# Value weights in buffers of their own, all early transfers asked for in order of use, aligned token rows, and another order of the last small operations

## The chip, the core and the metric

The kernel runs on one core of a Trainium2 chip. The time is the device time of one execution in microseconds. The profile's span is the stretch from the first to the last instruction in it; the profiled execution's own time is longer by what lies around the span. The engines are PE (matrix multiplication; PEld is its weight load), DVE (vector), ACT (scalar), POOL (general) and SP (asks for most transfers; ACT has a DMA queue of its own). PE works out of SBUF into eight banks of PSUM.

## The reference

256 tokens of width 1024 pass two layers. Everything is float32.

```
h = x
hn = rms_norm(h, g[0,0]);  h = h + stick_breaking_attention(hn, w_qkv, w_o)   # 16 heads of 64
h = h + sqrelu_mlp(rms_norm(h, g[0,1]), w1, w2)                               # 1024 -> 4096 -> 1024
shared = nsa_shared_kv(h, kv_norm, w_kv, cmp_pos, cmp_w1, cmp_w2)             # K/V of three branches
hn = rms_norm(h, g[1,0]);  h = h + nsa_attention(hn, w_q, gate_b, w_o, shared)
h = h + sqrelu_mlp(rms_norm(h, g[1,1]), w1, w2)
return rms_norm(h, final_norm)
```

In the first attention `qkv = hn @ w_qkv` with `w_qkv` of 1024 x 3072; its last third gives the values, 256 x 1024. Both ends of this program are what the change is about: the value projection, with which the kernel begins, and the final norm.

## The kernel before

A float32 product is made of three matmuls in a rounded type: each operand is split into a high part (`wh`, `xa` as `xn[0]`) and the remainder (`wl`, `xn[1]`), and high x high, low x high and high x low are added up in PSUM. For weights, `wh` is a cast, mostly on ACT, and `wl = raw - wh` a subtraction on DVE (`split`).

All weights form one list, `stream`, in the order of their use. `fetch` asks for the next entry on SP's queue and makes the coroutine that splits it. Raw weights lie in three buffers in turn (`tag="raw"`), split ones in three (`NB`). The next `fetch` is made when the second `wl` of a block has been issued, so a request stands on SP until DVE has freed the buffer.

The order of the instructions on DVE, ACT and POOL is set at build time by a planner (`Order`, `Chain`): it keeps a clock of its own, with costs such as `150 + 1.045 * m` for DVE, gives every chain of operations a rank and the time at which its data is expected (`ws.landed`), and issues whatever its model says can run. Each engine then runs its list in that order. PE's order is written out by hand.

`layer0` begins with eight matmuls on constants. Then the value projection runs over the eight blocks k of 128 input features: `v_first` for k=0 (two weight entries, `i_v0`, 512 columns each), `v_proj(i)` for the others, in pieces given by `V_CUT` as pairs (first k, how many k). For each k it takes the token rows, transposed, 128 features x 256 tokens (`xraw` from `in_xt`; `turned(k)` multiplies by the norm's gain and splits into `xa`) and twelve matmuls of 128x512 into four banks `pv`. `load(k0, k1)` asks for token rows: each row of `in_xt` begins with eight gains and goes on with 8 x 256 tokens, so block k begins at 32 + 1024 k bytes in a row of 8224. After the last k come `pr` (the row norms spread over a tile), and then `proj`, the q and k projections from `in_wqk`, one entry of 1024 KB for each pair of heads.

At the end of the second MLP `finish` is called for each finished quarter (token block t, column half n; the last quarter in two pieces of 256 columns). It issues the residual's square on ACT with a sum, the product with the final gain on DVE (`gain`), the running sum (`part`), and, after the last piece of a token block, the power -1/2 on POOL, the scaling by it in three pieces (384 columns on ACT, two of 320 on DVE) and three output transfers.

Of the kernel before, what the change touches and what calls it, by code (L numbers as in the profile page):

```python
# [8 lines left out]
F32 = mybir.dt.float32  # L9
# [18 lines left out]
V_CUT = ((1, 1), (2, 1), (3, 1), (4, 1), (5, 1), (6, 2))  # L28
# [143 lines left out]
def hybrid_kernel(ctx, tc, x, xt, eye, gcols, gfin, wqk, wv, wo0, wkv, wvs, wq, wg, wo1, w1, w2, cw1, cw2, cpos, gate_b, consts, out):  # L172
# [18 lines left out]
    def slot(i, shape, dt, name):  # L191
        return cp.tile(shape, dt, tag=f"e{i}", name=name, bufs=1)
# [51 lines left out]
    class Weights:  # L244
        raws, made, parts, gone, cur, landed = [], [], [], 0, -1, 0.0

    ws = Weights()
    ways = {"hi": "A"}

    def fetch():  # L250
        j = len(ws.raws)
        if j == len(stream):
            return
        src, n, whole = stream[j]
        raw = wp.tile([P, n], F32, tag="raw", name="raw", bufs=3)
        ws.raws.append(raw)
        ws.made.append(None)
        cuts = 2 if j == 0 else 1
        for c in range(cuts):
            r = slice(c * n // cuts, (c + 1) * n // cuts)  # L260
            nc.sync.dma_start(raw[:, r], src[:, r])
        for h in range(2):
            if h < cuts:
                ws.landed = max(o.t + 1900, ws.landed) + P * n * 4 / cuts / 330
            ws.parts.append(Chain(o, whole_part(j, h) if whole else split(j, h), rank_of(j), ws.landed))
# [9 lines left out]
    def split(j, half):  # L275
# [30 lines left out]
        if half:  # L306
            fetch()
# [246 lines left out]
    def layer0(ap):  # L554
# [6 lines left out]
        xg = slot(1, [P, NK + NK * T * P], F32, "xraw")  # L561
        xraw = xg[:, NK:].rearrange("p (k q) -> p k q", k=NK)
# [11 lines left out]
        def load(k0, k1):  # L574
            a, b = NK * (k0 > 0) + k0 * T * P, NK + k1 * T * P
            (nc.sync if k0 else nc.scalar).dma_start(xg[:, a:b], xt[:, a:b])
            ws.landed = max(o.t + 1900, ws.landed) + P * (k1 - k0) * 1024 / 330
            for k in range(k0, k1):
                in_x[k] = Chain(o, turned(k), 0.4, ws.landed)
# [31 lines left out]
        fetch()  # L611
        load(1, 2)
        fetch()
        load(2, 4)
        nc.scalar.dma_start(gc, gcols)
# [5 lines left out]
        load(4, 8)  # L621
# [6 lines left out]
        ws.landed = max(o.t + 1900, ws.landed) + 4500  # L628
        rstd = [None, None]
        rc = [Chain(o, rstd_of(t, rstd), 1.5, ws.landed) for t in range(T)]  # L630
# [3 lines left out]
        v_proj(5)  # L634
# [768 lines left out]
    last, gained = [[], []], [[], []]  # L1403
    ends = [[(0, 512)]] * 3 + [[(0, 256), (256, 512)]]

    def finish(i, q, c):
# [21 lines left out]
        def gen():  # L1428
            yield c
            gained[t].append(go(gain(), 0.3, 0))  # L1430
            yield act(m, lambda: nc.scalar.activation(sq[:, q], hres[t][:, q], AF.Square, accum_out=ss[:, k:k + 1]), 190)
            if k:
                yield last[t][k - 1]
            yield dve(1, lambda: nc.vector.tensor_scalar(part, ss[:, k:k + 1], part if k else D * EPS, None, op0=OP.add))
            if end:
                yield pool(1, lambda: nc.gpsimd.tensor_tensor(part, part, npow, op=OP.pow), 370)
# [43 lines left out]
def _layout(inp):  # L1480
# [6 lines left out]
    def blocks(w, nk, cw):  # L1487
# [14 lines left out]
        "xt": cont(np.concatenate([a["norm_gain"].reshape(4, D)[0].reshape(NK, P).T, a["x"][0].T.reshape(NK, P, T * P).transpose(1, 0, 2).reshape(P, NK * T * P)], 1)),  # L1502
# [39 lines left out]
```

## Time and profile before

| | us |
|---|---|
| median of 3 runs (lowest, highest) | 623.21 (623.17, 623.98) |
| time of the profiled execution | 623.1 |
| its span | 621.0 |
| PE busy in the span | 610.7 |
| DVE, ACT busy | 424.5, 328.3 |
| mean granted clock of PE, share of full | 0.998 |

In the views that follow a row of the timeline is: start, length, engine, line, operation, output<-input, shapes, how many were merged (x4), and in brackets the idle time of that engine just before and what ended it. A row "SPq" or "ACTq" is the time an engine takes to ask for transfers. "PE busy" lets a matmul end some 0.2 us after the next has begun, so the distance between starts, not the length, tells what one matmul costs. Requests of 128 x n float32 are n/2 KB.

### The profile page before, as it was taken

To read this page: it belongs to the slowest core of one execution; us is meant where nothing else is said; L and a number is where in the kernel's file an instruction comes from. 1 tells how busy PE (TensorE), PEld (TensorE's weight loads), DVE (VectorE), ACT (ScalarE), POOL (GpSimd) and SP (SyncE) were. 2 spreads that over 40 slices of the span, in tenths; PEclk is the share of its full clock that TensorE was granted. 3 is DMA by queue.
4 is the path that set the end of the run, shared out by engine and by line. 5 is a ranking of instruction groups with operands and counts; after the bars stand their busy time and mean duration, and the time that the engine had idled before them with its cause. 6 is when DMAs were issued, how large, how long until landed. Compare 5 with 4: busy or idle time off the path is not lost.

```text
span 621.0 us, 8967 instructions
## 1 busy us (share of the span) xinstructions
PE 610.7 (98%) x3580; PEld 513.4 (83%) x3580; DVE 424.5 (68%) x615; ACT 328.3 (53%) x563; POOL 41.2 (7%) x57
## 2 busy tenths in 40 slices
PE   8999999999999999999999999999999999999995
PEld 5799997888888888888887788677888888888884
DVE  4688996686656666555938999873876665566655
ACT  4657675464555444543906776452654554444432
POOL 0000000000000000000111542310000000000000
PEclk9999999999999999999999999999999999999999
DMA  7974425255554545555355363112365555455501
GB/s 260 369 283 158 142 99 179 86 220 195 203 205 172 188 183 203 204 176 218 140 203 204 136 204 137 69 69 102 137 218 197 194 194 212 163 191 189 204 1 68
DMA packets 17898, 108.24 MB, mean 174 GB/s; under 512 B 2368, under 2 KB 4160, under 8 KB 5696
## 3 DMA queue, kind: packets, MB, share of 16 engines
q1 hardware_dynamic: 17280, 107.11, 47.5%
q8 instruction: 28, 0.46, 0.3%
q10 hardware_dynamic: 576, 0.55, 0.3%
q14 instruction: 14, 0.11, 0.0%
HBM read 106.61 MB, written 1.05 MB: 173 GB/s over the span
## 4 chain that ended last, share of the span: by engine, by line
PE 82%; DVE 10%; DMA 3%; ACT 2%; issue 2%; SPq 0%; POOLq 0%; POOL 0%; DVEq 0%; ACTq 0%
PE acc L347 34%; PE pu L347 29%; PE qk L347 7%; DVE wl L299 4%; PE pk L347 4%; PE po L347 3%; PE z L347 2%; DMA raw<-in_wqk 1%; DVE nm L1084 1%; PE qp L347 1%; PE pt L359 1%; PE pa L359 1%; PE ptp L359 1%; DMA raw<-in_wv 1%; DMA xraw<-in_xt 1%
## 5 line engine op out<-in xcount | busy, mean ns | idle before, releaser
L299 DVE TENSOR_TENSOR wl<-raw,wh 128x1024 fp32r<-128x1024 f32 (+2 forms) x196 | 227.8, 1185 | 110.1 <-ACT wh L293 110.0
L293 ACT CAST wh<-raw 128x1024 fp32r<-128x1024 f32 (+2 forms) x196 | 193.9, 1018 | 116.7 <-PE acc L347 46.3
L347 PE MATMUL pu<-xn,wh 128*128 128x512 f32 x512 | 130.7, 394 | 0.0
L347 PEld LDWEIGHTS pu<-xn,wh 128*128 128x128 f32 x512 | 93.3, 188 | 18.7 <-issue 0.5
L347 PE MATMUL acc<-wh,hh 128*128 128x512 f32 (+1 forms) x256 | 99.7, 389 | 0.0
L347 PE MATMUL acc<-wl,hh 128*128 128x512 f32 (+1 forms) x256 | 99.6, 389 | 0.0
L347 PE MATMUL acc<-wh,hl 128*128 128x512 f32 (+1 forms) x256 | 99.4, 388 | 0.0
L347 PEld LDWEIGHTS pu<-xn,wl 128*128 128x128 f32 x512 | 70.8, 189 | 6.1
L347 PE MATMUL pu<-xn,wl 128*128 128x256 f32 x512 | 72.4, 281 | 0.0
L347 PEld LDWEIGHTS acc<-wh,hl 128*128 128x128 f32 x256 | 48.0, 188 | 10.0
L347 PEld LDWEIGHTS acc<-wh,hh 128*128 128x128 f32 x256 | 48.1, 188 | 9.1
L347 PEld LDWEIGHTS acc<-wl,hh 128*128 128x128 f32 x256 | 48.2, 188 | 8.9
L513 ACT CAST hh<-ms 128x512 fp32r<-128x512 f32 x32 | 19.9, 622 | 61.3 <-DVE ms L512 61.3
L347 PE MATMUL qk<-xa,wh 128*128 128x256 f32 x256 | 46.8, 285 | 0.0
L347 PE MATMUL acc<-wh,oT 128*128 128x512 f32 x128 | 43.7, 404 | 0.7 <-DVE oT L437 0.7
L347 PEld LDWEIGHTS qk<-xa,wh 128*128 128x128 f32 x256 | 39.2, 189 | 0.5 <-issue 0.3
L347 PE MATMUL qk<-xa,wl 128*128 128x256 f32 x128 | 36.1, 282 | 0.6 <-DVE wl L299 0.6
L499 ACT COPY mr<-pu 128x256 f32<-128x256 f32 x64 | 23.6, 369 | 24.2 <-PE pu L347 24.2
L514 DVE TENSOR_TENSOR hl<-ms,hh 128x512 fp32r<-128x512 f32 x32 | 22.1, 692 | 19.4 <-ACT hh L513 19.4
L347 PE MATMUL pk<-wh,xk 128*128 128x512 f32 (+1 forms) x128 | 33.6, 342 | 0.0
L1078 ACT ACTIVATE pe<-z,nm 128x256 f32<-128x256 f32 (+1 forms) x64 | 26.1, 428 | 12.7 <-DVE nm L1084 12.6
L347 PEld LDWEIGHTS acc<-wh,oT 128*128 128x128 f32 x128 | 24.0, 188 | 6.7 <-DVE oT L437 0.9
(178 smaller groups left out, 731.7 us busy)
## 6 DMA issues: line engine op xcount, KB each, us to landing
raw<-in_w SPq DMA_DIRECT2D x64, 1024.0 KB, 4.8
raw<-in_wqk SPq DMA_DIRECT2D x8, 1024.0 KB, 5.6
raw<-in_wo SPq DMA_DIRECT2D x8, 1024.0 KB, 4.8
raw<-in_wkv SPq DMA_DIRECT2D x4, 1024.0 KB, 4.9
raw<-in_cw SPq DMA_DIRECT2D x4, 1024.0 KB, 4.8
raw<-in_wq SPq DMA_DIRECT2D x4, 1024.0 KB, 4.9
raw<-in_wv SPq DMA_DIRECT2D x5, 512.0 KB, 5.0
raw<-in_wvs SPq DMA_DIRECT2D x2, 1024.0 KB, 5.0
```

Source lines behind the costliest of these rows:

```text
L293: nc.scalar.copy(ws.made[j][0][:, r], ws.raws[j][:, r])
L299: nc.vector.tensor_sub(ws.made[j][1][:, r], ws.raws[j][:, r], f32(ws.made[j][0][:, r]))
L347: nc.tensor.matmul(o_, a, b, start=first, stop=last, skip_group_check=True)
L359: nc.tensor.transpose(o_, a, i)
L499: yield act(256, lambda: nc.scalar.copy(r[:, q], pu[f][:, 256:512]))
L513: yield act(512, lambda: nc.scalar.copy(hh, sv))
L514: yield dve(512, lambda: nc.vector.tensor_sub(hl, sv, f32(hh)), port=True)
L1078: return act(n, lambda: nc.scalar.activation(d, z, AF.Exp, bias=nm[:, i:i + 1], accum_out=rs[:, t, hd, b:b + 1]), 150)
L1084: yield dve(256 * (t + 1), lambda: nc.vector.tensor_reduce(nm[:, i:i + 2], z, axis=AX.X, op=OP.max, negate=True))
```

## The change

Before the first matmul that needs data, the program now asks for all value weights, all token rows, the gains `gc`, x itself and the constants, and for three qk entries. The entries of the value weights have buffers of their own (`rv0` to `rv6`, in the pool of `layer0`), so they no longer wait for DVE; from the qk entries on the three `raw` buffers are used as before. Token rows of k=0 and k=1 go on ACT's queue, those of k=2 to 7 in pairs on SP's, between the weights. `gc` moves from ACT's queue to SP's. k=4 and k=5 form one entry; the third entry and the last two are asked for in two halves. The row of `in_xt` is filled up to 64 values ahead of the tokens, so a block begins at 256 + 1024 k bytes in a row of 8448. `lands` is a new model of when a transfer lands, for the planner only. In `finish`, the gains of a token block's last piece are issued after the running sum, and the scaling is one piece of 704 columns on DVE and 320 on ACT, with two transfers.

```diff
-V_CUT = ((1, 1), (2, 1), (3, 1), (4, 1), (5, 1), (6, 2))
+V_CUT = ((1, 1), (2, 1), (3, 1), (4, 2), (6, 2))
...
+    def lands(n):
+        ws.path = max(ws.path, o.t + 1100)
+        ws.path += n / (270 if ws.path < 10000 else 390)
+        ws.landed = ws.path + 1300
...
-        raw = wp.tile([P, n], F32, tag="raw", name="raw", bufs=3)
+        if j in i_v0 or j in i_v:
+            raw = ws.pool.tile([P, n], F32, name=f"rv{j}", bufs=1)
+        else:
+            raw = wp.tile([P, n], F32, tag="raw", name="raw", bufs=3)
-        cuts = 2 if j == 0 else 1
+        cuts = 2 if j in (0, 2) or j in i_v[-2:] else 1
...
-        if half:
+        if half and j > i_v[-1]:
             fetch()
...
-        xg = slot(1, [P, NK + NK * T * P], F32, "xraw")
+        xg = slot(1, [P, DH + NK * T * P], F32, "xraw")
...
-            (nc.sync if k0 else nc.scalar).dma_start(xg[:, a:b], xt[:, a:b])
+            (nc.sync if k0 > 1 else nc.scalar).dma_start(xg[:, a:b], xt[:, a:b])
...
         load(0, 1)
         fetch()
-        fetch()
         load(1, 2)
         fetch()
+        fetch()
         load(2, 4)
-        nc.scalar.dma_start(gc, gcols)
+        fetch()
+        fetch()
+        load(4, 6)
+        fetch()
+        load(6, 8)
+        fetch()
+        nc.sync.dma_start(gc, gcols)
+        for t in range(T):
+            nc.sync.dma_start(hres[t], x[t * P:(t + 1) * P, :])
+        nc.sync.dma_start(ident, eye)
+        nc.sync.dma_start(cst[:, 0:C_ROT], consts[:, 0:C_ROT])
...
+        for _ in range(3):
+            fetch()
...
         v_proj(1)
-        for t in range(T):
-            nc.sync.dma_start(hres[t], x[t * P:(t + 1) * P, :])
-        nc.sync.dma_start(ident, eye)
-        nc.sync.dma_start(cst[:, 0:C_ROT], consts[:, 0:C_ROT])
...
         def gen():
             yield c
-            gained[t].append(go(gain(), 0.3, 0))
+            late[t].append(gain)
+            if not end:
+                gained[t].append(go(late[t].pop()(), 0.3, 0))
...
             if end:
+                gained[t].extend(go(g(), 0.2, 0) for g in late[t])
...
-                yield [scaled("A", 640, 1024), scaled("D", 0, 320)]
-                yield [scaled("D", 320, 640)]
+                yield [scaled("A", 704, 1024), scaled("D", 0, 704)]
```

How this moves instructions, at three places. First SP's queue at the start of the program. In brackets stand the semaphores that a request waits for: DMAHW0 to DMAHW7 are eight counters that transfers take in turn and raise when they land, DVE_49 counts DVE's instructions. Before:

```order
L261 DMA raw_97<-in_wv 128x256 x2
L261 DMA raw_100<-in_wv 128x512
L576 DMA xraw_91<-in_xt 128x256
L261 DMA raw_103<-in_wv 128x1024
L576 DMA xraw_91<-in_xt 128x512
L261 DMA raw_125<-in_wv 128x1024 [waits DMAHW1_49,DMAHW0_49,DVE_49]
L261 DMA raw_138<-in_wv 128x1024 [waits DMAHW2_49,DVE_49]
L576 DMA xraw_91<-in_xt 128x1024
L261 DMA raw_160<-in_wv 128x1024 [waits DMAHW6_49,DMAHW3_49,DVE_49]
L261 DMA raw_182<-in_wv 128x1024 [waits DMAHW4_49,DMAHW0_49,DVE_49]
```

After:

```order
L269 DMA rv0_97<-in_wv 128x256 x2
L269 DMA rv1_101<-in_wv 128x512
L269 DMA rv2_103<-in_wv 128x512 x2
L585 DMA xraw_91<-in_xt 128x512
L269 DMA rv3_107<-in_wv 128x1024 [waits DMAHW0_49]
L269 DMA rv4_109<-in_wv 128x1024 [waits DMAHW1_49]
L585 DMA xraw_91<-in_xt 128x512 [waits DMAHW2_49]
L269 DMA rv5_112<-in_wv 128x1024 [waits DMAHW3_49]
L269 DMA rv5_112<-in_wv 128x1024 [waits DMAHW4_49]
L585 DMA xraw_91<-in_xt 128x512 [waits DMAHW5_49]
L269 DMA rv6_116<-in_wv 128x1024 [waits DMAHW6_49]
L269 DMA rv6_116<-in_wv 128x1024 [waits DMAHW7_49]
```

The token rows of k=1 (128x256) have left this queue, and no request there waits for DVE any more, only for the transfer eight places ahead of it.

Second, ACT at the same place: its two requests, then its first casts. Before:

```order
L576 DMA xraw_91<-in_xt 128x264
L615 DMA gc_70<-in_gcols 128x48
L293 CAST wh_111<-raw_97 128x256 [waits DMAHW0_49]
L293 CAST wh_111<-raw_97 128x256 [waits DMAHW1_49]
L293 CAST wh_121<-raw_100 128x256 [waits DMAHW2_49]
L293 CAST wh_121<-raw_100 128x256
L293 CAST wh_141<-raw_103 128x512 [waits DMAHW6_49]
L293 CAST wh_141<-raw_103 128x512
L568 ACTIVATE xa_89<-xraw_91 128x256 [waits DMAHW7_49,DMAHW3_49]
```

After:

```order
L585 DMA xraw_91<-in_xt 128x320
L585 DMA xraw_91<-in_xt 128x256
L301 CAST wh_135<-rv0_97 128x256 [waits DMAHW0_49]
L301 CAST wh_135<-rv0_97 128x256 [waits DMAHW1_49]
L577 ACTIVATE xa_89<-xraw_91 128x256 [waits DMAHW4_49,DMAHW3_49]
L301 CAST wh_152<-rv1_101 128x256 [waits DMAHW2_49]
L301 CAST wh_152<-rv1_101 128x256
L301 CAST wh_159<-rv2_103 128x512 [waits DMAHW5_49]
L301 CAST wh_159<-rv2_103 128x512 [waits DMAHW6_49]
```

The first operation on token rows k=1, which was DVE's (a TENSOR_SCALAR ahead of the second block's `wl`), is now ACT's, ahead of the second block's casts.

Third, DVE at the end, from the last quarter on. Before:

```order
L445 SCALAR_TENSOR_TENSOR hres1_73<-accz_5537,r2_4724,hres1_73 128x256 [waits DVE_49,PE_49]
L1434 TENSOR_SCALAR ssq1_4115<-ssq1_4115 128x1 [waits Activation_49]
L1425 SCALAR_TENSOR_TENSOR ys1_4117<-hres1_73,gf_4112 128x256
L1425 SCALAR_TENSOR_TENSOR ys1_4117<-hres1_73,gf_4112 128x256 [waits DVE_49]
L1434 TENSOR_SCALAR ssq1_4115<-ssq1_4115 128x1 [waits DVE_49,Activation_49]
L1420 TENSOR_SCALAR ys1_4117<-ys1_4117,ssq1_4115 128x320 [waits Pool_49]
L1420 TENSOR_SCALAR ys1_4117<-ys1_4117,ssq1_4115 128x320 [waits DVE_49]
```

After:

```order
L453 SCALAR_TENSOR_TENSOR hres1_73<-accz_5531,r2_4720,hres1_73 128x256 [waits DVE_49,PE_49]
L1451 TENSOR_SCALAR ssq1_4111<-ssq1_4111 128x1 [waits Activation_49]
L1440 SCALAR_TENSOR_TENSOR ys1_4113<-hres1_73,gf_4108 128x256
L1451 TENSOR_SCALAR ssq1_4111<-ssq1_4111 128x1 [waits DVE_49,Activation_49]
L1440 SCALAR_TENSOR_TENSOR ys1_4113<-hres1_73,gf_4108 128x256
L1435 TENSOR_SCALAR ys1_4113<-ys1_4113,ssq1_4111 128x704 [waits Pool_49]
```

One gain has gone behind the running sum, and one scaling has taken the place of two. PE's own order is the same from end to end. Between the two ends, the orders of DVE, ACT and POOL are the same but for layer 1, where the planner's clock has come to other choices: over the whole program one product `qw` has gone from POOL to DVE, one copy `pT` from DVE to ACT, and one half of `pe` from DVE to POOL.

More of the change, by code (lines that the diff above doesn't have):

```diff
@@ L244, in hybrid_kernel @@
     class Weights:
-        raws, made, parts, gone, cur, landed = [], [], [], 0, -1, 0.0
+        raws, made, parts, gone, cur, landed, path, pool = [], [], [], 0, -1, 0.0, 0.0, None
     ws = Weights()
     ways = {"hi": "A"}
+    def lands(n):
+        ws.path = max(ws.path, o.t + 1100)
+        ws.path += n / (270 if ws.path < 10000 else 390)
+        ws.landed = ws.path + 1300
     def fetch():
@@ L263, in fetch @@
             if h < cuts:
-                ws.landed = max(o.t + 1900, ws.landed) + P * n * 4 / cuts / 330
+                lands(P * n * 4 // cuts)
             ws.parts.append(Chain(o, whole_part(j, h) if whole else split(j, h), rank_of(j), ws.landed))
@@ L560, in layer0 @@
         v = slot(0, [P, T, D], F32, "v0")
-        xg = slot(1, [P, NK + NK * T * P], F32, "xraw")
-        xraw = xg[:, NK:].rearrange("p (k q) -> p k q", k=NK)
+        ws.pool = ap
+        xg = slot(1, [P, DH + NK * T * P], F32, "xraw")
+        xraw = xg[:, DH:].rearrange("p (k q) -> p k q", k=NK)
         pv = [[B(2 * n + t, f"pv{t}{n}") for n in range(2)] for t in range(T)]
@@ L574, in load @@
         def load(k0, k1):
-            a, b = NK * (k0 > 0) + k0 * T * P, NK + k1 * T * P
-            (nc.sync if k0 else nc.scalar).dma_start(xg[:, a:b], xt[:, a:b])
-            ws.landed = max(o.t + 1900, ws.landed) + P * (k1 - k0) * 1024 / 330
+            a, b = DH * (k0 > 0) + k0 * T * P, DH + k1 * T * P
+            (nc.sync if k0 > 1 else nc.scalar).dma_start(xg[:, a:b], xt[:, a:b])
+            lands(P * (k1 - k0) * 1024)
             for k in range(k0, k1):
@@ L610, in layer0 @@
         fetch()
-        fetch()
         load(1, 2)
         fetch()
+        fetch()
         load(2, 4)
-        nc.scalar.dma_start(gc, gcols)
+        fetch()
[9 more added lines that the diff above has]
+        nc.sync.dma_start(cst[:, 0:C_ROT], consts[:, 0:C_ROT])
+        lands(1250000)
+        rstd = [None, None]
+        rc = [Chain(o, rstd_of(t, rstd), 1.5, ws.landed) for t in range(T)]
+        for _ in range(3):
+            fetch()
         go_on = ap.tile([P, 2 * ROW], BF16, name="go_on", bufs=1)
@@ L620, in layer0 @@
         v_first(1)
-        load(4, 8)
         v_proj(0)
         v_proj(1)
-        for t in range(T):
-            nc.sync.dma_start(hres[t], x[t * P:(t + 1) * P, :])
-        nc.sync.dma_start(ident, eye)
-        nc.sync.dma_start(cst[:, 0:C_ROT], consts[:, 0:C_ROT])
-        ws.landed = max(o.t + 1900, ws.landed) + 4500
-        rstd = [None, None]
-        rc = [Chain(o, rstd_of(t, rstd), 1.5, ws.landed) for t in range(T)]
         v_proj(2)
@@ L633, in layer0 @@
         v_proj(4)
-        v_proj(5)
         o.need(*rc)
@@ L1402, in hybrid_kernel @@
     ys = [slot(1 + t, [P, 2, D], F32, f"ys{t}") for t in range(T)]
-    last, gained = [[], []], [[], []]
+    last, gained, late = [[], []], [[], []], [[], []]
     ends = [[(0, 512)]] * 3 + [[(0, 256), (256, 512)]]
@@ L1501, in _layout @@
         "x": cont(a["x"][0]),
-        "xt": cont(np.concatenate([a["norm_gain"].reshape(4, D)[0].reshape(NK, P).T, a["x"][0].T.reshape(NK, P, T * P).transpose(1, 0, 2).reshape(P, NK * T * P)], 1)),
+        "xt": cont(np.concatenate([a["norm_gain"].reshape(4, D)[0].reshape(NK, P).T, np.zeros((P, DH - NK), np.float32), a["x"][0].T.reshape(NK, P, T * P).transpose(1, 0, 2).reshape(P, NK * T * P)], 1)),
         "eye": np.eye(P, dtype=np.float32),
```

## The prediction

> **What bounds the kernel now.** I read the page's first part, then the list of what each engine waited for, then the timeline of the two ends. The first row of the page:
>
> ```profile
> PE 610.7 (98%) x3580; PEld 513.4 (83%) x3580; DVE 424.5 (68%) x615; ACT 328.3 (53%) x563; POOL 41.2 (7%) x57
> ```
>
> PE (the matmuls) is busy for 610.7 of 621.0 us. Whatever shortens the kernel must close a gap of PE, and there are few. The waits of PE over the whole span (us in total, times, longest):
>
> ```profile
> PE pv L347 <- DVE wl L299: 1.3, 1, 1.3
> ...
> PE acc L347 <- DVE oT L437: 0.7, 1, 0.7
> PE qk L347 <- DVE wl L299: 0.6, 1, 0.6
> PE ptp L359 <- DVE pT L1131: 0.2, 1, 0.2
> ```
>
> The first and third lie in the first 31 us, where the diff works; the others lie in layer 1. Now the first gap, in the timeline (start, length, engine, operation; in brackets what ended the idle time before it):
>
> ```profile
> 1.19 0.45 ACTq L615 DMA_DIRECT2D gc<-in_gcols  x1
> ...
> 2.11 0.43 SPq L576 DMA_DIRECT2D xraw<-in_xt  x1
> ...
> 5.29 0.72 ACT L293 CAST wh<-raw 128x256 fp32r<-128x256 f32 x2 [0.56 <-DMA raw<-in_wv]
> ...
> 6.09 1.15 PE L347 MATMUL pv<-wh,xa 128*128 128x512 f32 x4
> 7.06 0.35 DVE L569 TENSOR_SCALAR xa<-xraw 128x256 fp32r<-128x256 f32 x1 [1.63 <-DMA xraw<-in_xt]
> ...
> 8.06 0.42 DVE L299 TENSOR_TENSOR wl<-raw,wh 128x256 fp32r<-128x256 f32 x1
> 8.34 1.15 ACT L293 CAST wh<-raw 128x512 fp32r<-128x512 f32 x2 [2.33 <-DMA raw<-in_wv]
> 8.53 0.73 PE L347 MATMUL pv<-wl,xa 128*128 128x512 f32 x2 [1.28 <-DVE wl L299]
> ...
> 9.11 1.11 PE L347 MATMUL pv<-wh,xa 128*128 128x512 f32 x4
> 9.39 0.51 ACT L568 ACTIVATE xa<-xraw 128x256 fp32r<-128x256 f32 x1
> ...
> 11.92 1.09 PE L347 MATMUL pv<-wh,xa 128*128 128x512 f32 x4
> ```
>
> The two wl halves of the second weight block stand on DVE behind the first operation on token row block k=1, whose transfer, asked for at 2.1, lands only at 7.0. PE needs the last of them at 7.03 (6.09 and four matmuls of 0.233: from 9.11 to 11.92 twelve take 2.81) and gets it at 8.5. So k=1 begins at 9.1, k=2 at 11.92, and from there PE runs without a wait to the end of the value projection. Then the second gap:
>
> ```profile
> 22.50 1.06 ACT L381 ACTIVATE sq<-hres 128x1024 f32<-128x1024 f32 x1
> ...
> 27.75 1.99 ACT L293 CAST wh<-raw 128x1024 fp32r<-128x1024 f32 x2 [3.06 <-DMA raw<-in_wqk]
> 28.83 1.22 DVE L299 TENSOR_TENSOR wl<-raw,wh 128x1024 fp32r<-128x1024 f32 x1 [3.96 <-ACT wh L293]
> 29.07 0.48 PE L347 MATMUL qk<-xa,wh 128*128 128x256 f32 x2
> 30.11 0.39 PE L347 MATMUL qk<-xa,wl 128*128 128x256 f32 x1 [0.55 <-DVE wl L299]
> 30.33 0.40 PE L347 MATMUL qk<-xa,wh 128*128 128x256 f32 x2
> 30.57 0.28 PE L347 MATMUL qk<-xa,wl 128*128 128x256 f32 x1
> ```
>
> The first block of the qk weights lands at 27.7, and its first wl comes 2.4 us later, at 30.11. Two wh matmuls take 0.24 (30.33 to 30.57), so without a wait the wl matmul would have begun at 29.07 + 0.24 = 29.31: 0.8 us are lost there (the list counts 0.6, since it lets the matmuls before end late). What the transfers did meanwhile (busy time of each engine in a stretch; the last two numbers are the share of the 16 DMA engines and GB/s):
>
> ```profile
> 0.00:6.80 6.80, 5.99 (x21) 3.08 (x22) 1.51 (x4) 2.81 (x5) 1.10 (x7) 1.00 0.66 196
> 6.00:8.50 2.50, 1.25 (x6) 0.67 (x4) 1.42 (x4) 0.17 (x2) 0.00 (x0) 1.00 1.01 385
> 9.00:10.00 1.00, 1.00 (x6) 0.85 (x5) 1.00 (x3) 0.89 (x2) 0.00 (x0) 1.00 0.45 90
> 10.00:20.00 10.00, 10.00 (x44) 7.95 (x44) 8.26 (x17) 5.48 (x10) 0.00 (x0) 1.00 0.90 317
> 0.00:25.50 25.50, 23.41 (x95) 16.60 (x96) 14.87 (x31) 13.93 (x24) 2.20 (x11) 1.00 0.85 302
> 20.00:30.00 10.00, 9.56 (x45) 7.62 (x43) 3.84 (x7) 6.34 (x9) 1.23 (x5) 1.00 1.03 422
> 340.00:395.00 55.00, 54.07 (x431) 44.05 (x430) 53.28 (x103) 37.87 (x110) 24.18 (x18) 1.00 0.45 158
> ```
>
> And one transfer by itself (size, us from request to landing):
>
> ```profile
> gc<-in_gcols ACTq DMA_DIRECT2D x1, 24.0 KB, 3.3
> ```
>
> The stream runs dry at 9 to 10 us (90 GB/s): the weights have three buffers, and each further request waits for DVE to free one.
>
> **The change, part by part.** All times below are on the profiled span, 621.0, of an execution of 623.1; the median of the runs is 623.2, 0.1 above.
>
> (1) First gap. Three arrivals decide it. (a) Token rows k=1 go from the fourth place on SP to the second on ACT's queue, where gc lands at 1.19 + 3.3 = 4.5:
>
> That queue now carries 295 KB instead of 160, 135 more; at half of 385 GB/s, since SP's queue moves beside it, 0.7 us: landing at 5.2 (4.9 if it had all; 7.0 at worst, as now). ACT, not DVE, now takes the first operation on k=1 and stands there before it casts the second weight block: 5.2 + 0.05 + 0.5 (the ACTIVATE of 0.51) + 0.8 (5.29 to 6.09, two casts until PE starts) gives 6.55 for the four wh matmuls, 0.45 later than now; the wl are then in time, and k=0 ends at 6.55 + 0.93 + 0.47 = 7.95. (b) The third weight block, in two requests: its first half is complete after 131 + 131 + 262 + 164 + 131 + 262 = 1081 KB. The old stream had 196 x 6.8 = 1333 KB through at 6.8, so 1081 at 6.15. It had the old third block through at 6.8 (1339 KB) and ACT took it at 8.3, a lag of 1.5. So 7.65, a half cast of 0.57 and 0.1: k=1 at 8.3. (c) The fourth block is complete at 2129 KB: 6.8 + 796/385 = 8.9, plus 1.5 and 0.67, is 11.05 for k=2; PE arrives there at 8.3 + 2.8 = 11.1. Against 11.92 a gain of 0.8. From there the stream is ahead: the fifth block would be ready at 12.5 and is wanted at 13.9. Bounds: 1.5 (7.03 + 0.47 = 7.5 against 9.0 for k=1, a gain that (c) forbids unless the stream is quicker) and a loss of 0.7 (k=1 lands at 7.0: 7.0 + 1.35 + 1.4 = 9.75).
>
> (2) Second gap. PE would want the first wl at 29.31 - 0.8 = 28.5. Ahead of the first qk block there are now 4194 KB of value weights, 1081 of tokens, 25 of gains, 1049 of x, 66 and 237 of constants, 6650 KB; 5315 of them come after 6.8. Their rate is the open price: 385 in the one row without a break, 317 / 0.90 = 352 if the row from 10 to 20 us were full. I take 367, the middle, as both rows hold rows of the same 4 KB: 14.5 us, until 21.3. The block itself, 1049 KB at 422 (the row of 8 KB lines): 23.8. Lag: the old stream had its 7669 KB through at 25.4 (302 x 25.5 = 7701) and landed at 27.7, 2.2. So it lands at 26.0 and wl comes at 28.4, just when PE wants it. The gap of 0.8 closes: 30.11 becomes 28.5, and the two terms together give **1.6**. Bounds: 1.8 to 2.4 if the rate is 385 and (1) is better; with 352 the wl comes at 29.0, and 1.1 is left.
>
> The Trainium skill, DMA: Bandwidth & Descriptors, section "Where 436 GB/s comes from", holds that for HBM to SBUF the core's HBM share, some 358 GB/s, binds. With 358 throughout, the estimate is 1333 KB at 6.8, 6366 KB more until 24.6, landing at 26.8, wl at 29.2: a gain of 0.9 and 622.2 to 622.3. This trace disagrees, with 422 over ten us; so I give it no more than the chance of the slow stream below.
>
> (3) Requests no longer tied to DVE, V_CUT with one block of two k instead of two of one, gc and hres asked earlier or later: costs on SP are 0.43 a request with nothing else to do there; hres would land near 22, where now it is squared at 22.5, and is wanted before 28. The merged block is cast in 128x1024 pieces of 1.0 instead of 0.57 (27.75: two in 1.99), hidden by over 2 us of lead at k=4. Nothing.
>
> (4) The end. The last rows before, after the last matmul:
>
> ```profile
> 615.13 0.75 DVE L1425 SCALAR_TENSOR_TENSOR ys<-hres,gf 128x256 f32<-128x256 f32 x2
> 615.45 0.19 ACT L1431 ACTIVATION_READ_ACCUMULATOR ys<-hres 128x1 f32 x1
> 615.79 0.21 DVE L1434 TENSOR_SCALAR ssq<-ssq 128x1 f32<-128x1 f32 x1
> ...
> 616.66 0.68 DVE L1420 TENSOR_SCALAR ys<-ys,ssq 128x320 f32<-128x320 f32 x2 [0.66 <-POOL ssq L1436]
> 616.66 0.62 ACT L1418 ACTIVATE ys<-ys,ssq 128x384 f32<-128x384 f32 x1 [1.03 <-POOL ssq L1436]
> 617.08 0.81 SPq L1421 DMA_DIRECT2D out<-ys  x2
> ```
>
> The sum of squares waits behind both gains on DVE although ACT is done at 615.64; with one gain moved behind it, it starts at 615.67, 0.12 earlier, and the moved gain lies beside POOL's power. One DVE piece of 704 columns then takes 0.58 to 0.68 (two of 320 take 0.68): ready at 617.15, so the first request goes out 0.05 to 0.1 later than 617.08 and the last some 0.35 earlier than now (two requests in 0.81 from 617.08, so the second near 617.5).
>
> ```profile
> 618.00:619.00 1.00, 0.00 (x0) 0.00 (x0) 0.00 (x0) 0.00 (x0) 0.00 (x0) 1.00 1.02 363
> 619.00:620.00 1.00, 0.00 (x0) 0.00 (x0) 0.00 (x0) 0.00 (x0) 0.00 (x0) 0.50 0.40 140
> ```
>
> The 524 KB fill all 16 engines for 1.4 us (share 1.02), so what counts is when the first bytes start, not the last request. Between -0.35 and +0.1 I take **-0.05**, next to the full engines.
>
> (5) Layer 1. Its orders on DVE, ACT and POOL change because the planner's clock does: DVE gets one qw product from POOL, gives one pT copy to ACT and one half of pe to POOL. DVE is 53.3 of 55 us busy from 340 to 395, so a bad order would show at PE; but PE waits there 0.9 in all. I take 0, between -0.9 and +0.7 (one more wait like that for oT).
>
> Sum: 621.0 - 1.6 - 0.05 = 619.35, a time of 621.45 for the profiled execution and 621.5 for the median.
>
> **Rivals.**
> - The slow stream. With eight requests in flight the 4 KB rows move no faster than 352, and the first qk block takes back part: 1.1 gained at 352, and nothing at 5315 KB in 16.2 us, 328 GB/s (landing at 27.7 again). For it: 317 from 10 to 20 us with the engines 90% busy. Against: 422 and 385 elsewhere. Between these two rates 622.0 to 623.1.
> - Slower. The same place, a step further: if the stream goes on at 317 as in that row, 5315 KB end at 23.6, landing 28.3, wl at 30.7, 0.6 later than now; below 305 GB/s it costs over 1.2, at 300 the time is 624.6. Against it: the row holds waits of SP for DVE, which the change removes.
> - ACT stuck on k=1. If that transfer shares the DMA engines badly and lands at 7.0 as before, k=1 starts 0.7 later and the second gap's gain is eaten: 623.1, the change does nothing. For it: ACT now has this wait ahead of the second block's casts. Against: gc, at the same place in the same queue, landed at 4.5.
> - Layer 1 loses another wait of 0.7: 622.2. Or both waits there go and the stream is quicker: 620.3.
>
> **How the numbers follow.** About 0.2% (1.2 us) is what a measurement of this kernel can tell from no change. Forecast, 620.9 to 622.1: 0.50. Slow stream: 0.17. Slower: 0.06. ACT stuck: 0.05. Layer 1 worse: 0.10; better: 0.12. The range of 8 in 10 reaches from 620.3 to 622.9. Below 622.0 lie nine tenths of the forecast (0.45), the better layer 1 (0.12) and a quarter of the slow stream (0.04): 0.61 faster, 0.07 slower, 0.32 the same.
>
> **What would show it.** Step (1): PE's wait for wl before 9 us is gone or under 0.3, and the fourth group of twelve pv matmuls ends near 14. ACT's first xa operation starts near 5.3. Step (2): no wait of PE on qk at 28 us, the first qk cast at 26; GB/s near 370 or more without a hole from 6 to 24 us. Step (4): the last output request goes out near 617.2 less the shift. Layer 1: PE's waits there sum to 0.9. I am wrong if the first qk cast starts after 27, if ACT's first xa operation starts after 6, or if layer 1 shows new PE waits of over 0.7.

## The result, and the profile after

| | before | after |
|---|---|---|
| median us (lowest, highest) | 623.75 (623.17, 624.35), 6 runs | 619.50 (619.20, 619.64), 5 runs |
| time of the profiled execution | 623.1 | 619.5 |
| its span | 621.0 | 617.7 |
| accz to the end of the span | 7.58 | 7.79 |

The ratio of the times is 0.9932, with a 95% interval from 0.9918 to 0.9945. So the kernel became 4.2 us faster by the medians and 3.6 by the two profiled executions, where 1.7 was forecast; 619.5 lies below the range (620.3 to 622.9). One more execution of the kernel after took 1562.6 us; it was disturbed and counts nowhere here.

The first row of the page, and then the list of PE's waits, in full (us in total, times, longest):

```profile
PE 609.4 (99%) x3580; PEld 515.1 (83%) x3580; DVE 421.0 (68%) x609; ACT 330.0 (53%) x563; POOL 40.7 (7%) x57
```

```profile
PE warm L355 <- PEq L1549: 0.8, 1, 0.8
PE ptp L367 <- ACT pT L1146: 0.3, 1, 0.3
PE ptp L367 <- DVE pe L1121: 0.2, 1, 0.2
PE pv L355 <- DVE xa L578: 0.2, 1, 0.2
```

The row `warm` is the matmuls on constants, before the data. Both waits for wl are gone, and so is the one for oT. PE's busy time fell too, by 1.3 us with the same 3580 matmuls: the first sign of something that no step of the prediction held.

The head, in the timeline:

```profile
0.77 0.87 ACTq L585 DMA_DIRECT2D xraw<-in_xt  x2
...
4.77 0.51 ACT L577 ACTIVATE xa<-xraw 128x256 fp32r<-128x256 f32 x1
...
5.64 0.71 ACT L301 CAST wh<-rv 128x256 fp32r<-128x256 f32 x2 [0.35 <-DMA rv<-in_wv]
6.51 1.09 PE L355 MATMUL pv<-wh,xa 128*128 128x512 f32 x4
...
8.04 1.19 PE L355 MATMUL pv<-wh,xa 128*128 128x512 f32 x4
...
10.90 1.07 PE L355 MATMUL pv<-wh,xa 128*128 128x512 f32 x4
...
12.26 0.62 PE L355 MATMUL pv<-wh,xa 128*128 128x512 f32 x2
```

Step (1) said 6.55, 8.3 and 11.1 for the three matmul starts; they are at 6.51, 8.04 and 10.90. But the two casts at 5.64 that the first of them follows waited 0.35 for their own weights, not for the token rows k=1, which ACT had turned by 5.28. The rest of the head:

```profile
24.31 2.01 ACT L301 CAST wh<-raw 128x1024 fp32r<-128x1024 f32 x2 [2.70 <-DMA raw<-in_wqk]
...
27.22 0.61 PE L355 MATMUL pr<-ident,r 128*128 128x128 f32 x4
...
27.90 0.29 PE L355 MATMUL qk<-xa,wl 128*128 128x256 f32 x1
```

The first qk cast starts at 24.3 instead of 26.0, and the first qk matmul on wl at 27.90 instead of 28.5, with no wait. The rows by stretches (in order: PE, PEld, DVE, ACT, POOL busy, granted clock, DMA share, GB/s) answer to the prediction's open price:

```profile
9.00:10.00 1.00, 1.00 (x7) 0.79 (x6) 1.00 (x4) 0.21 (x1) 0.00 (x0) 1.00 0.99 381
10.00:20.00 10.00, 10.00 (x46) 8.29 (x45) 9.73 (x16) 8.21 (x11) 0.00 (x0) 1.00 1.04 408
0.00:25.50 25.50, 24.57 (x101) 18.33 (x102) 14.81 (x29) 15.88 (x25) 2.33 (x12) 1.00 0.94 357
340.00:395.00 55.00, 54.55 (x442) 44.44 (x444) 51.45 (x105) 39.59 (x115) 24.65 (x19) 1.00 0.42 154
```

The hole at 9 us (90 GB/s) is filled, and the ten us after it run at 408 GB/s, where 367 was taken. The last of the four rows is layer 1: DVE is busy for 51.45 instead of 53.28. The work stands some 2.5 us earlier in this kernel, so the same window is not the same work; at the same distance behind the first qp (337.54 to 392.54) DVE is busy for 52.00.

The end:

```profile
612.16 0.21 DVE L1451 TENSOR_SCALAR ssq<-ssq 128x1 f32<-128x1 f32 x1
612.29 0.41 DVE L1440 SCALAR_TENSOR_TENSOR ys<-hres,gf 128x256 f32<-128x256 f32 x1
612.45 0.66 POOL L1454 TENSOR_TENSOR ssq<-ssq,npow 128x1 f32<-128x1 f32 x1 [4.37 <-DVE ssq L1451]
613.14 0.56 ACT L1433 ACTIVATE ys<-ys,ssq 128x320 f32<-128x320 f32 x1 [1.02 <-POOL ssq L1454]
613.14 0.59 DVE L1435 TENSOR_SCALAR ys<-ys,ssq 128x704 f32<-128x704 f32 x1 [0.44 <-POOL ssq L1454]
613.74 0.38 ACTq L1436 DMA_DIRECT2D out<-ys  x1
613.76 0.34 SPq L1436 DMA_DIRECT2D out<-ys  x1
```

Here POOL's power takes 0.66 instead of 0.55, with the moved gain beside it on DVE. At the end of the first token block, where the gain has 512 columns, it takes 0.93:

```profile
606.99 0.68 DVE L1440 SCALAR_TENSOR_TENSOR ys<-hres,gf 128x512 f32<-128x512 f32 x1
607.16 0.93 POOL L1454 TENSOR_TENSOR ssq<-ssq,npow 128x1 f32<-128x1 f32 x1 [193.99 <-DVE ssq L1451]
```

To see where the 3.3 us of span come from, the two traces are cut at the first matmul of a kind, each read from the timeline:

| stretch (from the first matmul of one kind to that of the next) | before | after | change |
|---|---|---|---|
| start to qk on wl (the head) | 30.11 | 27.90 | -2.21 |
| to the first pu (q, k stage and attention of layer 0) | 86.50 | 86.83 | +0.33 |
| to the first pk (first MLP) | 178.91 | 178.29 | -0.62 |
| to the first qp | 25.54 | 25.58 | +0.04 |
| to the first pu of the second MLP (layer 1) | 115.07 | 113.99 | -1.08 |
| to the first accz (second MLP) | 177.29 | 177.32 | +0.03 |
| to the end of the span | 7.58 | 7.79 | +0.21 |

Three rows were not forecast: the first MLP, in which no instruction was moved, became faster; the q and k stage slower; and layer 1 gave 1.1.

### The profile page after: what moved, and what is told of

The parts are those of the page before. It is cut to its first block, busy times and chain, and to the rows that moved or that the text cites. A ratio compares the mean times of both kernels' runs of the same rounds, so it can differ in the third digit from the quotient of the medians.

```text
span 617.7 us, 8966 instructions
## 1 busy us (share of the span) xinstructions
PE 609.4 (99%) x3580; PEld 515.1 (83%) x3580; DVE 421.0 (68%) x609; ACT 330.0 (53%) x563; POOL 40.7 (7%) x57
## 4 chain that ended last, share of the span: by engine, by line
PE 95%; DMA 2%; ACT 1%; issue 1%; DVE 1%; POOL 0%; POOLq 0%; DVEq 0%; ACTq 0%
PE acc L355 35%; PE pu L355 29%; PE qk L355 8%; PE pk L355 5%; PE pv L355 4%; PE po L355 3%; PE z L355 3%; PE qp L355 3%; PE ptp L367 2%; DMA raw<-in_wq 1%; PE ph L355 1%; PE pt L367 1%; PE pa L367 1%; DMA xraw<-in_xt 1%; ACT pe L1093 0%
## 5 line engine op out<-in xcount | busy, mean ns | idle before, releaser
L307 DVE TENSOR_TENSOR wl<-raw,wh 128x1024 fp32r<-128x1024 f32 x180 | 216.1, 1221 | 105.0 <-ACT wh L301 105.0
L301 ACT CAST wh<-raw 128x1024 fp32r<-128x1024 f32 x180 | 184.7, 1052 | 108.4 <-PE acc L355 45.9
```

Source lines behind the costliest of these rows:

```text
L301: nc.scalar.copy(ws.made[j][0][:, r], ws.raws[j][:, r])
L307: nc.vector.tensor_sub(ws.made[j][1][:, r], ws.raws[j][:, r], f32(ws.made[j][0][:, r]))
```

## Experiments

The theory from these views: the head gained by the requests; the first MLP, and a part of the head, by new tile addresses (the longer `xraw` tile moves everything allocated behind it by 224 bytes); layer 1 by the new order on DVE, ACT and POOL; the end lost. Each experiment takes one of these alone. Unless said otherwise, a time is the median of 4 to 10 runs, and the kernel before, run in the same session on the same chip, had 623.6 to 623.7.

### Addresses alone, in the kernel before

```diff
-        xg = slot(1, [P, NK + NK * T * P], F32, "xraw")
-        xraw = xg[:, NK:].rearrange(...)
+        xg = slot(1, [P, DH + NK * T * P], F32, "xraw")
+        xraw = xg[:, NK:NK + NK * T * P].rearrange(...)
```

> The kernel before with one edit: the tile of the token rows is 8448 bytes a partition instead of 8224, so every tile allocated behind it (the split weights, xn of the first MLP, hh, hl and all of layer 1) lies 224 bytes higher, as in the changed kernel. The instructions and their orders on all engines are the same as before. Theory A (addresses): the changed kernel's quicker value projection (six matmuls in 1.36 us instead of 1.40) and first MLP (11.03 a block instead of 11.07), and its slower qk projection (three matmuls in 0.360 instead of 0.355), come from where the tiles lie; then this kernel shows 1.36, 11.03 and 0.360, and its span is 0.7 to 0.9 us below before, about 620.2. Theory B (the transfers or the orders of the other engines set the pace): it shows 1.40, 11.07, 0.355 and a span of 621.0.

Measured: 623.46 us (621.84 to 626.38), ratio 0.9995 (0.9980 to 1.0010). The time alone says nothing, since this kernel keeps the head of before, and its head scatters: in the profiled execution, the slowest of the ten, PE waited 0.97 and 0.76 for the first qk weights and the first qk on wl started only at 32.15. Just behind these waits, from 33.4 to 36.7, the granted clock was 0.50, and three qk matmuls took 0.64 instead of 0.36; the stretch to the first pu so became 88.42. No other profiled execution here shows such a drop inside the kernel. The later stretches do say something: the first MLP took 178.28, as after (178.29). In the expectation xn of the first MLP is among the tiles that move; it lies in the place of `xa`, ahead of `xraw`, and stays. The chain that ended last shows it group by group (start, length, what). First the kernel before, then this one:

```profile
134.50 5.45 PE acc L347 x24
139.95 5.62 PE pu L347 x32
```

```profile
138.40 5.47 PE acc L347 x24
143.86 5.56 PE pu L347 x32
```

In the first MLP every full group of 32 `pu` matmuls in the chain takes 5.62 before and 5.56 here, every 24 `acc` 5.45 or 5.46 and 5.47. In the second MLP, whose token operand lies behind `xraw` too and moves with the weights, `pu` takes 5.56 and `acc` 5.47 in both kernels. The instructions are the same; only addresses differ. Sixteen such pairs make -0.64, against -0.63 measured. Of a `pu` group it is the 16 matmuls on wh (128x512) that become faster, from 3.73 to 3.65 by their starts, while the 16 on wl (128x256) go from 1.89 to 1.91. The 0.02 of `acc` lies in the first six matmuls behind a `pu` group (1.37 and 1.39; the other 18 take 4.08 in both).

### The changed kernel without the filled rows

```diff
-        xg = slot(1, [P, DH + NK * T * P], F32, "xraw")
+        xg = slot(1, [P, NK + NK * T * P], F32, "xraw")
```

and the rows of `in_xt` without the filling, as before.

> The changed kernel without the filling: rows of the token array begin with eight gains again, so they are not aligned to 256 bytes, and all tiles lie where they lay before. Orders of all engines are those of the changed kernel. Theory A (addresses): matmuls fall back to 1.40, 11.07 and 0.355, and the span is 0.7 to 0.9 longer than the changed kernel's 617.7: 618.5. Theory B: 1.36, 11.03, 0.360 stay and the span is 617.7. Apart from that, if alignment matters to the transfer, the token rows of k=1 land later than 4.8 (ACT's first operation on them) by some 0.3 to 1 us, and PE gets a wait before 8 us; if it doesn't, the head is as in the changed kernel.

Measured: 620.52 us (620.44 to 620.54), span 618.7, ratio 0.9952 (0.9937 to 0.9966): 1.0 of the gain is lost. The first MLP is back at 178.90, its groups in the chain too:

```profile
138.42 5.62 PE pu L355 x32
144.04 5.45 PE acc L355 x24
```

and the first qk on wl starts at 28.68, its `pv` groups of six a distance of 1.40 apart, as before (1.36 after: 10.90 to 12.26 above). From there to the first pu this kernel is the quicker one, 86.40 against 86.83. Two things were mixed here, the filling and the addresses; the next three part them.

### Which offset counts

Let the offset be the address of a tile modulo 64 bytes. In the kernel before, `xa` (which is also the first MLP's input `xn[0]`) lies at 32 and `wh`, `wl` at 0; in the kernel after all three lie at 32. Eight more columns behind `xraw` put the weights at 0; a `npow` tile of nine columns instead of one, ahead of `xa`, moves all of them by 32 bytes. The rows stay filled in all three.

```diff
# weights moved
-        xg = slot(1, [P, DH + NK * T * P], F32, "xraw")
+        xg = slot(1, [P, DH + NK * T * P + 8], F32, "xraw")
# both moved
-    npow = cp.tile([P, 1], F32, name="npow")
+    npow_ = cp.tile([P, 9], F32, name="npow")
+    npow = npow_[:, 0:1]
# xa moved: both edits
```

> The changed kernel with 32 more bytes behind the token rows' tile, so that every tile behind it starts at a multiple of 64 bytes again (as before the change), and the tiles ahead of it (xa, and xq in layer 1) stay at 32 past one. Orders and transfers are those of the changed kernel. Theory A1 (offset within 64 bytes sets the pace of PE): six pv matmuls take 1.40 us instead of 1.36, a block of the first MLP 11.07 instead of 11.03, three qk matmuls 0.355 instead of 0.360; span 618.4 to 618.7. Theory A2 (some larger unit of the address counts, which 32 bytes don't change): 1.36, 11.03, 0.360, span 617.7.

> The changed kernel with 32 bytes more ahead of xa, so that all large tiles, xa and xq too, start at multiples of 64 bytes. Theory A1 has two forms. If the weights' offset alone counts, paces are those of offset 0: 1.40, 11.07, 0.355, span 618.4 to 618.7. If both operands count, pv (stationary xa, moving wh) and qk (stationary wh, moving xa) change again, by up to 0.04 for six matmuls and 0.005 for three, and the second MLP (moving xn in xa's place) changes from 11.03 a block; the first MLP, whose operands are both at 0 as before the change, is at 11.07. Theory A2: 617.7.

> The changed kernel with 32 bytes more ahead of xa and 32 more behind the token rows: xa and xq at multiples of 64, the weights and all tiles behind the token rows at 32 past one. If the weights' offset alone counts: 1.36, 11.03, 0.360 as in the changed kernel, span 617.7. If both count: the first MLP is at 11.03 (both operands as in the changed kernel), and pv, qk and the second MLP (11.03 now) differ, in the second MLP by up to 0.04 a block, 0.6 us in all.

| xa at, weights at | us | span | six pv | first MLP | q, k stage and attention |
|---|---|---|---|---|---|
| 32, 32 (after) | 619.50 | 617.7 | 1.36 | 178.29 | 86.83 |
| 0, 0 | 619.35 | 617.6 | 1.36 to 1.38 | 178.24 | 86.84 |
| 32, 0 | 620.37 | 618.7 | 1.40 | 178.91 | 86.39 |
| 0, 32 | 620.35 | 618.7 | 1.40 | 178.89 | 86.38 |

Among these four it counts whether the two operands have the same offset, not which. With the same one the value projection and the first MLP are faster and the q and k stage is slower, 1.0 us in the sum. The second MLP takes 177.3 in all four: its token operand moves with the weights, and not, as two of the expectations had it, with `xa`. The filled rows by themselves give no time: the kernel at (32, 0) has them, the one of the section before has not, and both have a span of 618.7. They do let the rows of k=1 land sooner (3.2 to 3.5 us from request to landing, 4.3 without the filling), but the trace puts no wait of ACT or PE down to them.

### The order of layer 1, put in and taken out

In the kernel before, the new model `lands` in the place of the old one; in the kernel after, the old model. DVE, ACT and POOL then have in layer 1 the order of after and of before.

```diff
# in the kernel before
-                ws.landed = max(o.t + 1900, ws.landed) + P * n * 4 / cuts / 330
+                lands(P * n * 4 // cuts)
# in the kernel after, the other way round
```

> The kernel before with only the planner's model of landing times replaced by that of the changed kernel. No transfer is moved. In layer 1 the orders of DVE, ACT and POOL are then those of the changed kernel; at the start one operation on token rows k=1 moves from DVE to ACT and some wl move. Theory C (layer 1's order): the 0.9 us that the changed kernel is quicker between the first q projection (321.13 before) and the output projection (396.34 before), 75.2 against 74.3, come with the order; PE's wait of 0.7 for oT goes, span 620.1 if the head costs the same. Rival D: they come from addresses or from the other phase of the weight transfers; then 75.2 stays and the span is 621.0. The head may lose up to 0.7 where ACT now waits for k=1's rows, which still land at 7.0.

> The changed kernel with the planner's old model of landing, all else as changed; DVE's, ACT's and POOL's orders in layer 1 are then those of before. Theory (the order of layer 1 alone is worth 1.0): from the first qp to the first pu of the second MLP 115.0 instead of 114.0, PE waits 0.7 for oT again, span 618.7 (plus or minus 0.2 by the head, whose order on ACT and DVE moves by a few rows too), time 620.5. Rival (the 1.0 comes from when weights land, or from the shifted tiles): 114.0, no wait for oT, span 617.7.

Measured: the kernel before with the new order 622.78 us, ratio 0.9983 (0.9974 to 0.9993), and layer 1 takes 114.08 instead of 115.07 (in this execution the head took 31.81, so that its span of 621.7 says nothing). The kernel after with the old order 620.60 (620.38 to 621.10), span 618.5, layer 1 114.92. So the order of layer 1 is worth 1.0 us from either side. PE's waits of the last:

```profile
PE acc L355 <- DVE oT L445: 0.7, 1, 0.7
PE ptp L367 <- DVE pT L1146: 0.2, 1, 0.2
```

Why, the chain that ended last of the kernel before tells (the stretch in which PE waits for oT):

```profile
383.29 0.69 DVE pe L1106
383.98 0.60 DVE pT L1131
...
385.62 0.61 DVE qm L1036
...
386.98 0.76 DVE qw L1038
387.74 3.30 DVE wl L299 x2
391.04 0.60 DVE oT L437
391.64 1.20 DVE nm L1084 x2
392.83 0.33 DVE sct L1224
393.17 0.61 DVE pT L1131
...
393.82 0.65 PE ptp L359 x4
```

The path ran along DVE here, not along PE. The same place after:

```profile
388.52 0.59 PE ptp L367 x4
389.11 1.39 PE acc L355 x6
390.50 0.22 PE psct L367 x2
390.73 0.44 PE ptp L367 x4
391.16 1.40 PE acc L355 x6
```

It runs along PE. In the chain of the whole kernel before, DVE, with shorter pieces of ACT, carries the path from 327.05 to 393.78; in the one after, PE carries it from 348.73 on. Between the first qp and the first of these `acc`, DVE is busy for less with the new order: it has one copy of pT (0.61) and one half of pe fewer and a qw product (0.68) more, and the same 16 wl take 19.7 us instead of 20.9, with the longest at 1.75 instead of 2.31 (2.29 in the changed kernel with the old order, 1.75 in the kernel before with the new one). That longest one is the second of the two at 387.74, just ahead of the oT; beside it POOL's qw and qm products take 2.14 and 2.13, where after no wl stands beside that qm, and it takes 1.27. So part of the gain is likely not work taken from DVE but a wl that no longer falls beside POOL's qm. That the order is worth 1.0 is shown from both sides; how the 1.0 divides among these pieces is read from the chain, and no run takes one of them alone.

### Token rows k=1 in SP's queue

The changed kernel, with k=1 as the third request of SP instead of the second of ACT.

```diff
-            (nc.sync if k0 > 1 else nc.scalar).dma_start(xg[:, a:b], xt[:, a:b])
+            (nc.sync if k0 else nc.scalar).dma_start(xg[:, a:b], xt[:, a:b])
```

> The changed kernel with the token rows of k=1 on SP's queue, third there, ahead of the second weight block, instead of on ACT's. Everything else is the same; ACT still stands in wait for them ahead of that block's casts. They were taken at 4.77 us on ACT's queue. Theory G (the queue of its own closes the first gap): they now come with the second block, at 5.5 to 6, the four wh matmuls of that block start at 7 instead of 6.5, and PE waits 0.3 to 0.6 before k=1: span 618.1 to 618.3. Rival H (the order of the requests alone does it, since both queues share the same engines): no wait of PE over 0.2 and 617.7.

Measured: 621.13 us (620.16 to 622.61), ratio 0.9960 (0.9947 to 0.9973), 1.6 slower than the changed kernel, and more than was expected. The timeline:

```profile
5.06 0.51 ACT L577 ACTIVATE xa<-xraw 128x256 fp32r<-128x256 f32 x1 [0.57 <-DMA xraw<-in_xt]
...
7.41 1.91 ACT L301 CAST wh<-rv 128x256 fp32r<-128x256 f32 x4 [1.84 <-DMA rv<-in_wv]
...
8.17 1.19 PE L355 MATMUL pv<-wh,xa 128*128 128x512 f32 x4 [2.04 <-ACT wh L301]
```

The token rows are taken nearly as soon (5.06 against 4.77); it is the second weight block, now behind them in the same queue, that is cast at 7.41 instead of 5.64, and PE waits 2.0 for it. So the queue of its own was worth 1.6 us by the medians, and the eight times (620.16 to 622.61) lie clear of those of the changed kernel. That it comes by what the queue lets through behind these rows is what this one trace shows; how much of it is scatter is open, since with the requests unmoved the same cast starts anywhere from 5.4 to 6.9 in the other profiled executions.

### The end, alone and taken back

The new `finish` in the kernel before, the old one in the kernel after, and, in the second kernel of the next section, the old order of the gains with the single piece of 704.

```diff
# the kernel after with the old finish
-            late[t].append(gain)
-            if not end:
-                gained[t].append(go(late[t].pop()(), 0.3, 0))
+            gained[t].append(go(gain(), 0.3, 0))
...
-                gained[t].extend(go(g(), 0.2, 0) for g in late[t])
...
-                yield [scaled("A", 704, 1024), scaled("D", 0, 704)]
+                yield [scaled("A", 640, 1024), scaled("D", 0, 320)]
+                yield [scaled("D", 320, 640)]
```

> The kernel before with only the new end (gain behind the running sum, one scaling of 704 columns on DVE, two output transfers). From the start of the last matmuls (first of the last 48 acc matmuls) to the end of the span it was 23.1 us before and 23.3 in the changed kernel. Theory E: the end as such costs 0.1 to 0.2, since POOL's power runs beside the moved gain on DVE and takes 0.66 instead of 0.55 (and 0.93 beside a gain of 512 columns for the first token block), and the outputs start later: span 621.1 to 621.2. Rival F: the end saves the 0.05 forecast and the 0.2 are scatter between runs: 620.9 to 621.0, power 0.55.

> The changed kernel with the final operations of before (gains on DVE as soon as issued, scaling in 384 on ACT and two of 320 on DVE, three output requests). Theory (the new tail costs, since DVE's gain lies beside POOL's power and lengthens it from 0.55 to 0.66 and 0.93): from the last kind of matmul, accz, to the end of the span 7.58 again instead of 7.79, span 617.5, time 0.2 below the changed kernel's 619.5. Rival, the step as predicted (the new tail gains 0.05): 617.75, within 0.1 of the changed kernel.

Measured: 623.13 us, ratio 0.9992 (0.9983 to 1.0001), for the first; 619.19 (618.66 to 619.73) and a span of 617.3 for the second. By their times neither is told apart from the kernel it is made from. The stretch from accz to the end tells more, over all kernels: with the old end 7.58, 7.59, 7.55 and 7.32; with the single piece 7.66 to 7.91 in ten kernels. The two sets don't overlap, and their means lie 0.26 apart (0.20 without the 7.32). The first output request stands 3.65 to 3.66 behind the first accz where it could be read with the old end, and 3.81 to 3.84 with the new one. In the kernel after with the old end the last rows are

```profile
612.63 0.55 POOL L1451 TENSOR_TENSOR ssq<-ssq,npow 128x1 f32<-128x1 f32 x1 [4.86 <-DVE ssq L1449]
...
613.63 0.81 SPq L1436 DMA_DIRECT2D out<-ys  x2
```

Its first output request stands 3.65 behind the first accz matmul (609.98), in the kernel after 3.83 (613.74 - 609.91). In the kernel before it stands 3.66 behind, and yet the end took 7.58 there and 7.32 here: 0.26 is also what two executions with the same requests at the end differ by.

### A version that should have beaten both

64 bytes more in each `wh` and `wl` tile, and the q and k weights 32 bytes further in, so that the offsets differ in the q and k stage alone; then the same with the old order of the gains and the single piece of 704.

```diff
-                    ws.made[j] = (wp.tile([P, n], F32R, tag="wh", name="wh", bufs=NB),
-                                  wp.tile([P, n], F32R, tag="wl", name="wl", bufs=NB))
+                    off = 8 if j in i_qk else 0
+                    w = [wp.tile([P, n + 16], F32R, tag=t, name=t, bufs=NB) for t in ("wh", "wl")]
+                    ws.made[j] = tuple(x[:, off:off + n] for x in w)
```

> The changed kernel with 64 bytes more in each of the tiles wh and wl, and the q and k weights written 32 bytes further into them, so that their offset differs from the token operand's by 32 bytes (modulo 64) in that stage alone. Theory of the offsets (pv and the first MLP want equal offsets, the stage of the q and k projections wants different ones): from the first qk wl matmul to the first pu 86.4 instead of 86.8, all else as in the changed kernel: span 617.3. Rival (it is not the offsets of these operands but where other tiles lie, or the whole layout): 86.8 and 617.7; or other stages change by several tenths because everything behind wh has moved.

> As the kernel with the q and k weights shifted by 32 bytes, and the gains of the last pieces issued as before ahead of the running sum, but the scaling in 704 columns on DVE and 320 on ACT as in the change. If the order of the gains alone costs the 0.2 of the tail and the offsets 0.4: accz to the end 7.5 to 7.6, span 617.0 to 617.1, time 618.8. If the single piece of 704 costs it: accz to the end stays at 7.8, span 617.3.

Measured: 621.85 us (621.29 to 622.51), span 619.4, and 621.93 (621.52 to 622.95), span 621.1: both 2.4 slower than the changed kernel. From the first qk on wl to the first acc the shift gave what was expected (58.95 instead of 59.30 us, and 58.87 at offsets 32 and 0); to the first pu, where the expectation set 86.4, it is 86.70, since the `acc` behind became slower. And the first MLP took 179.21 and the second 178.29, 0.9 and 1.0 more, and the stretch between first pk and first qp 25.93 instead of 25.58, though in the two MLPs all offsets modulo 64 are equal. The rival of the expectation held. The chain of the first of the two:

```profile
154.41 5.50 PE acc L356 x24
159.91 5.56 PE pu L356 x32
165.47 5.51 PE acc L356 x24
170.98 5.63 PE pu L356 x32
```

One `pu` group in three takes 5.63, in step with the three buffers of `wh`, which are no longer 8192 but 8256 bytes apart; and the `acc` groups take 5.49 to 5.51. So "equal modulo 64" is not the whole rule. Equal modulo 128 would fit every `pu` group of all runs (of the three buffers here one differs from `xn` modulo 128), but that was worked out afterwards and not tried by itself, and it doesn't tell why `acc` became slower.

The second kernel does settle the end: with the gains in their old order POOL's power is at 0.55 again, and the stretch from accz to the end is 7.87 all the same, its first request 3.84 behind accz. So the order of the gains is not what costs, but the new cut of the scaling: one piece of 704 on DVE and two requests. (Its span of 621.1 has in it a head in which PE waits 1.0 for a cast; the other runs of it had 619.6 to 620.4.)

No version beat the changed kernel by more than the runs scatter: the one with the old end (619.19) and the one at offsets 0 and 0 (619.35) lie within its 619.2 to 619.64.

## Why the prediction was wrong, step by step

- **Steps (1) and (2), the head.** The mechanism was right and the size nearly so, in part by luck: step (1) let ACT stand for the rows of k=1, landing at 5.2, but they were there for ACT by 4.77, and it was the second weight block that held the casts to 5.64, so that 6.51 beside 6.55 comes from another wait than the one that was counted. With the offsets of before (no filled rows), the first qk on wl started at 28.68, 1.43 earlier than before; 1.6 was predicted. The rate of the stream was put too low (367; measured 408 for ten us), and the first qk block came 1.7 earlier than said, but that could give nothing more: PE was no longer waiting for it. The rule of the Trainium skill quoted there (DMA: Bandwidth & Descriptors, "Where 436 GB/s comes from") is not what this trace of a kernel on one core shows, with 408 where it holds that some 358 binds. The slow stream, and with it the slower rival, is out; so is ACT stuck on k=1 (4.77, not 7.0).
- **The term that was missing.** The sum has no term for the filled rows but their bytes (the 295 KB on ACT's queue). They made a tile longer, moved the tiles behind it, and so changed the pace of PE, by 1.0 us in the sum of three stages (618.7 against 617.7). The prediction took PE's busy time as fixed where it didn't wait. This and step (5) are the steps that failed: without either of the two gains the kernel takes 620.5 (620.52 without the filling) or 620.6 (620.60 with the old order), inside the range, and with both 619.5.
- **Step (5), layer 1.** Put at 0, measured -1.0 from both sides, just beyond its bounds (-0.9). The step read PE's waits there, 0.9 in all, and had the new order before it, a copy of pT and a half of pe less on DVE; but it didn't follow the chain of waits, which ran along DVE, with shorter pieces of ACT, for over sixty us ahead of that very wait. By that chain, work taken from DVE is a likely gain and not a coin's toss. And it counted operations, not their lengths: the wl of 2.31 beside POOL's products (1.21 is the median) is a delay that a count doesn't show. The rival in which both waits go had 0.12.
- **Step (4), the end.** -0.05 was predicted and +0.2 measured. The sum of squares did start 0.12 earlier (2.25 behind accz instead of 2.37). But the moved gain did not lie freely beside POOL's power: the power took 0.66 instead of 0.55, and 0.93 beside the longer gain, so the scaling starts 3.23 behind accz as before (3.24). The Trainium skill, SBUF — State Buffer, section "Who interferes with whom", has the rule: a DVE instruction with two SBUF inputs contends with a GpSimd instruction that reads SBUF. These rows agree with it in kind. Then the single piece of 704 makes the first request 0.18 later, where the step said 0.05 to 0.1, and by its own argument (what counts is when the first bytes start) that is most of the loss; the rest lies within what the ends of two executions differ by.
- **Step (3)** came out at nothing, as far as the runs tell: no wait of PE is left in the head that a request sets. No run takes it alone.
- **The base.** The median of before was taken from three runs, 623.2; over all sessions it is 623.6 to 623.75, and the profiled execution of before was one of its best. Kernels with the old requests scatter from 621.2 to 626.4, the head by itself from 30.1 to 32.2 at the first qk on wl; those with the new requests as they are, the two with larger `wh` tiles aside, stay within 0.1 to 1.1 us. One drop of the granted clock, told under the addresses, is part of that scatter in one execution. So the change gives more against the median than against the profile: 0.65 of the 4.25 is this, and 0.3 more is time outside the span (2.1 before, 1.8 after), which no step looked at.

By the two profiled executions the sum reads: head 1.43, offsets 1.0, layer 1 1.0, end -0.2, together 3.2 of the 3.3 us of span.

## What to carry to other kernels

When a change makes a tile longer, everything allocated behind it moves: compare the pace of a long run of equal matmuls (one group in the chain, 5.62 against 5.56) in a stage that the change doesn't touch, before the difference is put down to anything else. A wait of the bounding engine should be followed back along the chain: where that chain runs on another engine for tens of microseconds, each operation that the change adds to or takes from that engine in that stretch is likely on the path, and is not "beside" it. And a scaling piece that ends in a transfer is better cut so that the first request goes out early; one piece less saved DVE 0.1 here and cost 0.18 to the first request.

## What the runs showed of the hardware that was not expected

The pace of a matmul depends on where its two operands lie in SBUF relative to each other, by 1% in `pu` (5.62 against 5.56 for 32) and 3% in `pv` (1.40 against 1.36 for six), and the other way round in the q and k stage (86.39 against 86.83 us). The sign goes with the width here: the matmuls of 128x512 (`pv`, and `pu` on wh) are faster with equal offsets, those of 128x256 (`qk`, and `pu` on wl) slower; no run changes the width alone. The 0.02 of the `acc` groups (5.45 against 5.47) is not shown to be such a case, since both operands of `acc` lie behind `xraw` and moved together, and only its first six matmuls behind a `pu` group changed. The Trainium skill, in the same table of SBUF — State Buffer, gives the moving operand and the weight load of PE read ports that are independent of each other. From that one would not expect relative addresses to matter; these runs show that they do, by 1.0 us of 618. Which addresses agree with which, beyond a step of 32 bytes, stays open.
